# Score products of two heads in alternation between the halves of the array, and a decode result turned by 128-column transposes

## The chip, the cores and the metric

The kernel runs on one core of a Trainium2 chip. The metric is the device time of one execution in microseconds (us). Before the change it is 2710.97 us, the median of three runs (2708.78 to 2711.12). One further execution was profiled; every row of the trace is from that one. In the rows, PE is the matrix engine (TensorE), PEld its weight loads, DVE the vector engine, ACT the scalar engine, POOL GpSimd, and SP the engine that issues DMAs. L139 is line 139 of the kernel.

## The reference, cut to what matters

One layer of an encoder on 512 prompt frames and on eight decode streams of 16 frames, with float32 values throughout:

```
qa, ka, va, qb, kb, vb = split(rmsnorm(x) @ w_in)      # 16 heads A; 16 query, 2 key/value heads B; head size 64
A: softmax(qa ka^T / 8 + bias[distance]) va            # own chunk of 64 frames and the eight before
B: softmax(rope(qb) rope(kb)^T / 8, with a sink) vb    # own chunk and the two before
x = x + [rms(A) | rms(B)] @ w_out
y = rmsnorm(x + (silu(h @ w_gate) * (h @ w_up)) @ w_down),  h = rmsnorm(x)
```

The decode frames do the same against cached keys and values. The keys and values of the frames are outputs too.

## The kernel before

**Products.** A float32 operand is split into a high and a low part (`split`, L137: ACT makes the high part at L138, DVE the rest at L139), and one product is three matmuls, high by high, high by low and low by high (`mm3`, L145, lines 147, 148 and 149), or two where one operand is exact enough (`mm2`, L151, lines 154 and 155). Wherever such a helper records an operation, its line stands for all callers.

**Stages.** First the joint projection: 26 blocks of 128 columns, each through `dense` (L165), which goes over 16 blocks `k` of the contraction and issues six matmuls of 320 columns for each. Blocks 24 and 25 (keys and values of B) come first; then, for p from 0 to 7, `project_b(2p)` and `project_b(2p+1)` while p is below 4, and `project_a(p)` with three blocks. Then w_out (lines 714 and 772), and the feed-forward part, by far the longest.

**Attention inside the projections.** `dense` calls `pump` after each `k`, so once in six matmuls. `pump` (L72) takes the next of its streams and runs the generator that is active there up to its next `yield`. Up to p = 4 there are two streams, "heads 0" and "heads 1", which draw from one queue; from p = 4 on one stream takes heads and the other decode work. `heads_of` (L429) queues one generator per head, `prompt_a` (L361) or `prompt_b` (L397); `rr` is the parity of the head: an even head's 64 rows of q and k lie on partitions 0 to 63, an odd one's on 64 to 127.

A generator of A takes eleven turns: fetch the bias; scores of the query blocks 0 and 3; of 1 and 2; softmax; three empty turns; transposes of weights (`flip`, L348) in two turns; the rest of them and the first product with v; the other products. One of B takes ten. Scores (`scores`, L325) of block i are one `mm3` into one PSUM bank, 128(i+1) columns wide for A and at most 256 for B, and a DVE operation (L330) that adds the bias and takes the maximum. PSUM buffers for all this come from a pool of four banks (`bank`, L131); `dense` has its own.

`n.get` and `n.put` hand out named SBUF slots. List S has 62; 7 serve as constants, 3 for projection results, 32 hold the normalised input until the projections end, and 4 go to the queries of B, so 16 are left for heads and decode work. When a list is empty, `get` calls `pump` until another generator gives a slot back.

**Decode.** `decode_b` and `decode_a(0)` are added at p = 4, `decode_a(1)` before w_out. Ahead of w_out stands `n.drain_queue("decode")` (L708), which pumps without a projection beside it until the first two are done. `decode_a` makes for each of eight streams a block `od` with eight heads beside each other and needs, of column group t, 32 columns turned: four matmuls against a slice of the identity (L615) give 32 columns each in one bank, and two DVE copies (L620) pick 16 of each.

The order of the instructions on each engine isn't that of the source: it is chosen when the program is built, among the instructions that count as ready by then, with the source's order as priority. The first fence of the prediction that shows `x2` is an instance.

Of the kernel before, what the change touches and what calls it, by code (L numbers as in the profile page):

```python
# [8 lines left out]
ALU = mybir.AluOpType  # L9
# [4 lines left out]
P = 128  # L14
# [4 lines left out]
SP = 512  # L19
# [3 lines left out]
DS = 16  # L23
# [26 lines left out]
class Net:  # L50


    def __init__(self, nc, tc, io, pools):
        self.nc, self.tc, self.io, self.pools = nc, tc, io, pools
        self.uid = 0
        self.lists = {"S": [f"S{i}" for i in range(N_S)], "W": [f"W{i}" for i in range(N_W)]}
        self.owner, self.turns = {}, {}
        self.queues, self.active, self.turn = {}, {}, 0
        self.streams = (("heads 0", "heads"), ("heads 1", "heads"))

    def nm(self, s):
        self.uid += 1
# [159 lines left out]
def sh(t, *shape):  # L222
    v = t[:, :int(np.prod(shape))]
    if len(shape) == 2:
        v = v.rearrange("p (a b) -> p a b", a=shape[0])
    elif len(shape) == 3:
        v = v.rearrange("p (a b c) -> p a b c", a=shape[0], b=shape[1])
    return v


def r(ap):
    return ap.bitcast(F32R)


def build(nc, tc, io, pools):
    n = Net(nc, tc, io, pools)
    dma = nc.sync.dma_start
# [4 lines left out]
    def col(k):  # L242
        c0[0] += k
        return cst[:, c0[0] - k:c0[0]]
# [3 lines left out]
    sinks, sink_d = col(16), col(2)  # L248
# [4 lines left out]
    def tr(out, src):  # L253
        nc.tensor.transpose(out, src, n.ident)  # L254
# [21 lines left out]
    kb = (r(kb0), r(kb1))  # L276
# [6 lines left out]
    first = []  # L283
    for kt in range(KT):
        if kt in START_CHUNKS:
            idx, k0, k1, lst = START_CHUNKS[kt]
# [3 lines left out]
        own, hl = pair("S")  # L290
# [31 lines left out]
        return out  # L322


    def scores(q, k, rr, i, k0, k1, bias, s, mx):  # L325
        ps = n.bank()[:, :k1 - k0]
        rows = slice(64 * rr, 64 * rr + 64)
        qs, ks = slice(128 * i, 128 * i + 128), slice(k0, k1)
        n.mm3(ps, (q[0][rows, qs], q[1][rows, qs]), (k[0][rows, ks], k[1][rows, ks]), True, True)
        nc.vector.tensor_tensor_reduce(s, ps, bias, 1.0, -3e38, ALU.add, ALU.max, mx)  # L330

    def softmax(ss, mx, sink):
        nm, den = n.small(4), n.small(4)
        if sink is None:
            nc.vector.tensor_scalar(nm, mx, -1.0, None, ALU.mult)
        else:
            nc.vector.tensor_scalar(nm, mx, sink, -1.0, ALU.max, ALU.mult)
        for i, s in enumerate(ss):
            nc.scalar.activation(s, s, AF.Exp, bias=nm[:, i:i + 1], accum_out=den[:, i:i + 1])
        if sink is not None:  # L340
            se = n.small(4)
            nc.scalar.activation(se, nm, AF.Exp, bias=sink)
            nc.vector.tensor_tensor(den, den, se, ALU.add)
        nc.vector.reciprocal(den, den)
        for i, s in enumerate(ss):
            nc.vector.tensor_scalar(s, s, den[:, i:i + 1], None, ALU.mult)
# [11 lines left out]
        n.split(ps, *hl)  # L358
        return own, hl

    def prompt_a(h, q, k, v, ot, done):  # L361
        rr = h % 2
        bias, t0, t1 = n.get("S"), n.get("S"), n.get("S")
        dma(out=bias[:, :SP], in_=io["bias_a"][h])
        yield
        es = [t0[:, 512:640], t1[:, :256], t1[:, 256:640], t0[:, :512]]
        mx = n.small(4)
        for pick in ((0, 3), (1, 2)):
            for i in pick:
                scores(q, k, rr, i, 0, P * (i + 1), bias[:, SP - P * (i + 1):SP], es[i], mx[:, i:i + 1])  # L370
            yield
        softmax(es, mx, None)
        n.put("S", bias)
        yield
        yield
        yield
        yield
        blk = lambda i, j: es[i][:, P * j:P * j + P]
        o0, p0 = flip([blk(i, 0) for i in range(4)], "S")
        yield  # L380
        o1, p13 = flip([blk(i, 1) for i in range(1, 4)] + [blk(3, 3)], "S")
        yield
        ps = n.bank()
        vr = v[rr]
        n.mm2(ps, vr[:, 0:128], p0, True, False)
        n.put("S", *o0)
        o2, p2 = flip([blk(i, 2) for i in range(2, 4)], "S")
        n.put("S", t0, t1)
        yield
        n.mm2(ps[:, 128:], vr[:, 128:256], cut(p13, 0, 384), False, False)  # L390
        n.mm2(ps[:, 384:], vr[:, 384:512], cut(p13, 384, 512), False, False)
        n.mm2(ps[:, 256:], vr[:, 256:384], p2, False, True)
        n.put("S", *o1, *o2)
        both(ot, rr, ps)
        done()

    def prompt_b(t, rr, q, ot, done):  # L397
        sink = sinks[:, 8 * rr + t:8 * rr + t + 1]
        t0, t1 = n.get("S"), n.get("S")
        es = [t0[:, 512:640], t0[:, :256], t0[:, 256:512], t1[:, :256]]  # L400
        mx = n.small(4)
        for pick in ((0, 1), (2, 3)):
            for i in pick:
                k0 = max(0, i - 1) * P
                w = (i + 1) * P - k0
                scores(q, kb, rr, i, k0, k0 + w, mask_b[:, 256 - w:], es[i], mx[:, i:i + 1])
            yield
        softmax(es, mx, sink)
        yield
        yield  # L410
        yield
        yield
        oa, pa = flip([es[0], es[1][:, :P], es[2][:, P:], es[3][:, :P]], "S")
        yield
        ob, pb = flip([es[1][:, P:], es[2][:, :P], es[3][:, P:]], "S")
        n.put("S", t0, t1)
        yield
        ps = n.bank()
        vr = r((vb0, vb1)[rr])
        n.mm2(ps[:, 0:256], vr[:, 0:128], cut(pa, 0, 256), True, False)  # L420
        n.mm2(ps[:, 256:512], vr[:, 256:384], cut(pa, 256, 512), False, False)
        yield
        n.mm2(ps[:, 128:384], vr[:, 128:256], cut(pb, 0, 256), False, False)
        n.mm2(ps[:, 384:512], vr[:, 384:512], cut(pb, 256, 384), False, True)
        n.put("S", *oa, *ob)
        both(ot, rr, ps)
        done()

    def heads_of(kind, p, held, *args):  # L429
        ot = n.get("S")  # L430
        left = [2]

        def done():
            left[0] -= 1
            if not left[0]:
                dma(out=(oa_d if kind is prompt_a else ob_d)[p, :, :SP], in_=ot[:, :SP])
                n.put("S", ot)
                for lst, t in held:
                    n.put(lst, t)

        for rr in range(2):
            n.add("heads", kind(*((2 * p + rr,) if kind is prompt_a else (p, rr)), *args, ot, done))

    def rope(x):
        rot = n.get("S")
# [88 lines left out]
    def decode_a(g):  # L534
        o_s, bias, z = n.get("D"), n.get("D"), (n.get("D"), n.get("D"))
# [4 lines left out]
        for i in range(3):  # L540
            s, two = n.get("S"), (n.get("D"), n.get("D"))
# [5 lines left out]
            else:  # L547
                ps = n.bank().rearrange("p (a b) -> p a b", a=4)
# [7 lines left out]
        for b in range(NB):  # L556
            own = slice(DS * b, DS * b + DS)
            for e in range(2):
                zv = r(sh(z[e], 4, 160))
                for rr in range(2):  # L560
                    rows = slice(64 * rr, 64 * rr + 64)
# [5 lines left out]
            ps = n.bank()[:, :CA + DS]  # L567
            for hf in range(2):
# [7 lines left out]
                for j in range(2):  # L576
                    t = 2 * hf + j
# [3 lines left out]
            mx, den, d2 = n.small(1), n.small(1), n.small(1)  # L581
            s, pt = n.get("S"), n.get("S")
# [27 lines left out]
            od = n.get("S")  # L610
            nc.vector.tensor_scalar(od[:, :512], po, den, None, ALU.mult)
            yield
            pf = n.bank()[:, :P].rearrange("p (t c) -> p t c", t=4)
            for t in range(4):
                nc.tensor.matmul(pf[:, t], od[:, P * t:P * t + P], n.ident[:, 32 * t:32 * t + 32],  # L615
                                 start=True, stop=True)
            n.put("S", od)
            for rr in range(2):
                rows = slice(64 * rr, 64 * rr + 64)
                nc.vector.tensor_copy(sh(o_s, 4, P)[rows, :, own], pf[rows, :, DS * rr:DS * rr + DS])  # L620
        dma(out=oa_d[4 * g:4 * g + 4, :, SP:].rearrange("t p c -> p t c"), in_=sh(o_s, 4, P))
        n.put("D", o_s, bias, *z, *held)

# [12 lines left out]
    ps = n.bank()[:, :P]  # L636
# [38 lines left out]
    for p in range(8):  # L675
        if p < 4:
            project_b(2 * p)
            project_b(2 * p + 1)
        if p == 4:
            while len(n.lists["Q"]) < 4:  # L680
                n.pump()
            n.move("Q", "D", 4)
            n.put("D", cos, sin)
            while n.active.get("heads 1"):
                n.pump()
            n.streams = (("heads 0", "heads"), ("decode", "decode"))
            n.add("decode", decode_b())
            n.add("decode", decode_a(0))
        project_a(p)
# [24 lines left out]
    for m in range(KT):  # L714
        ps = n.dense([(io["w_out_b"][m], 8)], acts_b)
        if m == 0:
            n.rstd(ssq, 1024, r_b)
        xr, x = n.get("S"), n.get("S")
# [53 lines left out]
    for i, m in enumerate(m for kt in range(8) for m in (kt, kt + 8)):  # L772
        ps = n.dense([(io["w_out_a"][m], 8)], acts_a)
# [103 lines left out]
    for i in range(NPAIR):  # L877
        for src in ("w_gate", "w_up"):
# [4 lines left out]
            start, end = i == 0 and src == "w_gate", i == NPAIR - 1 and src == "w_up"  # L883
# [29 lines left out]
            else:  # L913
                for x, g in zip(y, gate):
                    nc.vector.tensor_tensor(x, x, g, ALU.mult)
                u, w = gate
# [211 lines left out]
```

## Time and profile before

| what | value |
|---|---|
| median of the runs | 2710.97 us |
| the profiled execution's own time | 2706.72 us |
| its span, first to last instruction | 2705.0 us |
| PE busy, DVE busy, ACT busy | 97%, 71%, 40% of the span |
| mean granted clock of PE | 0.986 |
| score products (64 rows, L147 to L149, w/o decode) | first at 81.2 us, last at 735 us |
| L615, the turning of the decode result | 128 instructions, 558.1 to 846.2 us |

A row of the timeline has the start in us, the duration in us, the engine, the line, the operation, output and inputs, the part of the array as rows x columns, the size of the moving operand, and a count of merged instructions. A duration of a matmul contains its filling and draining, so matmuls overlap; what one costs is the distance from its start to the next start.

### The profile page before, as it was taken

Reading aid. Unit: us, or ns where it says so; the run is one execution under the profiler, and the core shown is the slowest. Engines: PE = TensorE matmul, PEld = TensorE weight load, DVE = VectorE, ACT = ScalarE, POOL = GpSimd, SP = SyncE. Lnnn points to the kernel's source line nnn. Section 1 sums busy time; section 2 is a strip of 40 time slices with the busy share of each in tenths; the row PEclk is TensorE's granted clock in tenths of the full one; section 3 lists DMA queues with packets and bytes.
Section 4 is the critical chain, followed back from the end, with each engine's and each line's share of the span. In section 5 each row is a group of like instructions: output and inputs, shape, how many; then the busy total and the mean of one; then the engine's idle time right before and its main releaser. Section 6 shows DMA issues by size and latency. Waiting matters only on the chain.

```text
span 2705.0 us, 44972 instructions
## 1 busy us (share of the span) xinstructions
PE 2629.3 (97%) x17629; PEld 2568.5 (95%) x17629; DVE 1928.6 (71%) x2956; ACT 1084.0 (40%) x1759; POOL 786.9 (29%) x564
## 2 busy tenths in 40 slices
PE   7999999999999999999999999999999999999986
PEld 7999999999899999999999999999999899999986
DVE  7565565665766777667767666676668888888897
ACT  4333343444633553333333333333334444444443
POOL 3000000000211123343333333433334534444453
PEclk9999999999999999999999999999999899999997
DMA  5222223333556443333333333333335644444344
GB/s 166 85 73 82 89 68 108 109 119 114 183 187 217 147 134 104 104 119 103 105 115 108 108 121 100 119 102 109 113 106 173 214 130 127 132 133 130 107 116 135
DMA packets 154147, 332.23 MB, mean 123 GB/s; under 512 B 18064, under 2 KB 69264, under 8 KB 153936
## 3 DMA queue, kind: packets, MB, share of 16 engines
q1 hardware_dynamic: 153936, 329.38, 38.8%
q8 instruction: 138, 2.26, 0.4%
q14 instruction: 73, 0.60, 0.1%
HBM read 274.38 MB, written 54.20 MB: 121 GB/s over the span
## 4 chain that ended last, share of the span: by engine, by line
PE 84%; DVE 8%; DMA 4%; issue 3%; ACT 2%; SPq 0%; DVEq 0%; POOL 0%; ACTq 0%
PE dn L147 18%; PE dn L149 17%; PE dn L148 17%; PE at L147 9%; PE at L149 9%; PE at L148 9%; DVE W L139 2%; PE at L254 1%; DVE S L847 1%; DMA S<-act_d 1%; DMA W<-w_down 1%; DVE S L139 1%; PE at L155 1%; PE at L154 1%; DVE S L1018 0%
## 5 line engine op out<-in xcount | busy, mean ns | idle before, releaser
L147 PE MATMUL dn<-S,W 128*128 128x320 f32 x3694 | 1165.9, 316 | 15.4 <-DVE S L847 9.6
L149 PE MATMUL dn<-S,W 128*128 128x320 f32 x3694 | 1152.1, 312 | 14.0 <-DVE W L139 13.8
L148 PE MATMUL dn<-S,W 128*128 128x320 f32 x3694 | 1150.3, 311 | 1.1 <-DVE S L139 1.1
L138 ACT ACTIVATE W<-W 128x1024 fp32r<-128x1024 f32 (+2 forms) x632 | 609.3, 965 | 1045.1 <-PE dn L148 518.0
L139 DVE TENSOR_TENSOR W<-W,W 128x1024 fp32r<-128x1024 f32 (+2 forms) x632 | 768.3, 1216 | 126.6 <-ACT W L138 122.3
L147 PEld LDWEIGHTS dn<-S,W 128*128 128x128 f32 x3694 | 700.6, 190 | 33.2 <-issue 16.9
L149 PEld LDWEIGHTS dn<-S,W 128*128 128x128 f32 x3694 | 700.3, 190 | 19.4 <-DVE W L139 18.9
L148 PEld LDWEIGHTS dn<-S,W 128*128 128x128 f32 x3694 | 701.1, 190 | 3.0 <-DVE S L139 1.3
L149 PE MATMUL at<-S,W 128*128 128x320 f32 x1594 | 494.4, 310 | 7.0 <-DVE W L139 6.6
L147 PE MATMUL at<-S,W 128*128 128x320 f32 x1594 | 493.5, 310 | 1.5 <-ACT W L138 1.5
L148 PE MATMUL at<-S,W 128*128 128x320 f32 x1594 | 493.0, 309 | 0.0
L830 POOL TENSOR_TENSOR W<-W,W 128x1024 f32<-128x1024 f32 (+2 forms) x76 | 162.5, 2138 | 588.0 <-DVE W L139 519.0
L149 PEld LDWEIGHTS at<-S,W 128*128 128x128 f32 x1594 | 299.5, 188 | 10.2 <-DVE W L139 10.2
L147 PEld LDWEIGHTS at<-S,W 128*128 128x128 f32 x1594 | 299.9, 188 | 1.7 <-ACT W L138 1.7
L148 PEld LDWEIGHTS at<-S,W 128*128 128x128 f32 x1594 | 299.6, 188 | 0.0
L847 DVE TENSOR_TENSOR S<-S,dn 128x320 f32<-128x320 f32 x358 | 164.2, 482 | 97.6 <-PE dn L149 97.6
L826 DVE TENSOR_TENSOR W<-W,W 128x1024 f32<-128x1024 f32 (+2 forms) x76 | 134.5, 1770 | 103.9 <-DMA W<-w_up 52.4
L837 POOL TENSOR_TENSOR W<-W,W 128x1024 f32<-128x1024 f32 (+2 forms) x76 | 165.5, 2178 | 111.9 <-DVE W L139 106.5
L847 DVE TENSOR_TENSOR S<-S,at 128x320 f32<-128x320 f32 x262 | 123.5, 481 | 70.1 <-PE at L149 70.0
L218 POOL TENSOR_TENSOR S<-S,S 128x640 f32<-128x640 f32 x40 | 75.7, 1893 | 155.5 <-ACT S L217 155.1
L828 DVE TENSOR_TENSOR W<-W,W 128x1024 f32<-128x1024 f32 (+2 forms) x76 | 82.9, 1091 | 30.7 <-DMA W<-w_gate 24.1
L139 DVE TENSOR_TENSOR S<-at,S 128x512 fp32r<-128x512 f32 (+2 forms) x109 | 64.1, 600 | 50.3 <-ACT S L138 49.9
(149 smaller groups left out, 2351.0 us busy)
## 6 DMA issues: line engine op xcount, KB each, us to landing
W<-w_gate SPq DMA_DIRECT2D x88, 512.0 KB
W<-w_up SPq DMA_DIRECT2D x88, 512.0 KB
W<-w_in SPq DMA_DIRECT2D x66, 512.0 KB
W<-w_down SPq DMA_DIRECT2D x64, 384.0 KB
W<-w_down SPq DMA_DIRECT2D x68, 320.0 KB
act_d<-S SPq DMA_DIRECT2D x66, 320.0 KB
half<-act_d SPq DMA_DIRECT2D x81, 160.0 KB
S<-act_d SPq DMA_DIRECT2D x80, 160.0 KB
```

Of the source, the lines that this page charges most:

```text
L138: self.nc.scalar.activation(hi, src, AF.Identity)
L139: self.nc.vector.tensor_tensor(lo, src, f(hi), ALU.subtract)
L147: mm(out, a[0], b[0], start=first, stop=False)
L148: mm(out, a[0], b[1], start=False, stop=False)
L149: mm(out, a[1], b[0], start=False, stop=last)
L154: mm(out, a, b[0], start=first, stop=False)
L218: (eng or nc.gpsimd).tensor_tensor(ssq, ssq, sq, ALU.add)
L826: nc.vector.tensor_tensor(b12[:, w], b12[:, w], b22[:, w], sub)
L828: nc.vector.tensor_tensor(s6[:, w], b11[:, w], b12[:, w], sub)
L830: nc.gpsimd.tensor_tensor(b11[:, w], b22[:, w], s6[:, w], sub)
L837: nc.gpsimd.tensor_tensor(b21[:, w], b21[:, w], s6[:, w], sub)
L847: add = lambda o, a, b: nc.vector.tensor_tensor(o, a, b, ALU.add)
```

## The change

A generator now serves two heads, an even and an odd one. `scores` takes both, gets two banks, and issues the six matmuls in alternation, so that neighbours in the order use different halves of the array's rows. Blocks of A go from the widest to the narrowest, one block of both heads per turn. The softmax of the two heads takes two turns; two empty turns follow (there were three); the tails of the two heads take turns (`in_turn`). There is one stream of heads up to p = 4, where there were two, and the wait for "heads 1" at p = 4 goes.

The decode result is turned by four plain 128-column transposes into a whole bank, and the two copies read the wanted 16 columns of each group through a view with a step of 160 columns (`diagonal`).

```
-        self.streams = (("heads 0", "heads"), ("heads 1", "heads"))
+        self.streams = (("heads 0", "heads"),)
...
+def diagonal(ap, first):
+
+    return bass.AP(tensor=ap.tensor, offset=ap.offset + first, ap=[list(ap.ap[0]), [160, 4], [1, DS]])
...
-    def scores(q, k, rr, i, k0, k1, bias, s, mx):
-        ps = n.bank()[:, :k1 - k0]
-        rows = slice(64 * rr, 64 * rr + 64)
+    def scores(q, k, i, k0, k1, biases, ss, mxs):
+
+        pss = [n.bank()[:, :k1 - k0] for _ in range(2)]
         qs, ks = slice(128 * i, 128 * i + 128), slice(k0, k1)
-        n.mm3(ps, (q[0][rows, qs], q[1][rows, qs]), (k[0][rows, ks], k[1][rows, ks]), True, True)
-        nc.vector.tensor_tensor_reduce(s, ps, bias, 1.0, -3e38, ALU.add, ALU.max, mx)
+        for x, (a, b) in enumerate(((0, 0), (0, 1), (1, 0))):
+            for rr, ps in enumerate(pss):
+                rows = slice(64 * rr, 64 * rr + 64)
+                nc.tensor.matmul(ps, q[a][rows, qs], k[b][rows, ks], start=x == 0, stop=x == 2)
+        for ps, bias, s, mx in zip(pss, biases, ss, mxs):
+            nc.vector.tensor_tensor_reduce(s, ps, bias, 1.0, -3e38, ALU.add, ALU.max, mx[:, i:i + 1])
+
+    def in_turn(works):
+
+        while works:
+            for w in list(works):
+                try:
+                    next(w)
+                    yield
+                except StopIteration:
+                    works.remove(w)
...
+        for i in (3, 2, 1, 0):
+            w = P * (i + 1)
+            scores(q, k, i, 0, w, [x[:, SP - w:SP] for x in biases], [h[1][i] for h in heads], [h[2] for h in heads])
+            yield
+        n.put("S", *biases)
+        for _, es, mx in heads:
+            softmax(es, mx, None)
+            yield
         yield
         yield
-        yield
-        yield
+        yield from in_turn([tail_a(rr, own, es, v, ot, done) for rr, (own, es, _) in enumerate(heads)])
...
-            pf = n.bank()[:, :P].rearrange("p (t c) -> p t c", t=4)
+            pf = n.bank()
             for t in range(4):
-                nc.tensor.matmul(pf[:, t], od[:, P * t:P * t + P], n.ident[:, 32 * t:32 * t + 32],
-                                 start=True, stop=True)
+                tr(pf[:, P * t:P * t + P], od[:, P * t:P * t + P])
...
-                nc.vector.tensor_copy(sh(o_s, 4, P)[rows, :, own], pf[rows, :, DS * rr:DS * rr + DS])
+                nc.vector.tensor_copy(sh(o_s, 4, P)[rows, :, own], diagonal(pf[rows], DS * rr))
...
-            while n.active.get("heads 1"):
-                n.pump()
```

`prompt_b` is changed in the same way as `prompt_a`, with blocks 0 to 3 in this order. Turns per pair of heads: 16 for A (two generators of eleven before) and 15 for B (two of ten).

More of the change, by code (lines that the diff above doesn't have):

```diff
@@ L359, in flip, with prompt_a, tail_a @@
         return own, hl
[L361 to L364, printed above, removed]
+    def prompt_a(p, q, k, v, ot, done):
+        biases = n.get("S"), n.get("S")
+        for rr, bias in enumerate(biases):
+            dma(out=bias[:, :SP], in_=io["bias_a"][2 * p + rr])
         yield
[L366 to L370, printed above, removed]
+        heads = []
+        for rr in range(2):
+            t0, t1 = n.get("S"), n.get("S")
+            heads.append(((t0, t1), [t0[:, 512:640], t1[:, :256], t1[:, 256:640], t0[:, :512]], n.small(4)))
+        for i in (3, 2, 1, 0):
+            w = P * (i + 1)
+            scores(q, k, i, 0, w, [x[:, SP - w:SP] for x in biases], [h[1][i] for h in heads], [h[2] for h in heads])
             yield
-        softmax(es, mx, None)
-        n.put("S", bias)
+        n.put("S", *biases)
+        for _, es, mx in heads:
+            softmax(es, mx, None)
+            yield
         yield
         yield
-        yield
-        yield
+        yield from in_turn([tail_a(rr, own, es, v, ot, done) for rr, (own, es, _) in enumerate(heads)])
+    def tail_a(rr, own, es, v, ot, done):
         blk = lambda i, j: es[i][:, P * j:P * j + P]
@@ L387, in prompt_a @@
         o2, p2 = flip([blk(i, 2) for i in range(2, 4)], "S")
-        n.put("S", t0, t1)
+        n.put("S", *own)
         yield
@@ L395, in prompt_a, with prompt_b, tail_b @@
         done()
[L397 to L406, printed above, removed]
+    def prompt_b(t, q, ot, done):
+        heads = []
+        for rr in range(2):
+            t0, t1 = n.get("S"), n.get("S")
+            heads.append(((t0, t1), [t0[:, 512:640], t0[:, :256], t0[:, 256:512], t1[:, :256]], n.small(4)))
+        for i in range(4):
+            k0 = max(0, i - 1) * P
+            w = (i + 1) * P - k0
+            scores(q, kb, i, k0, k0 + w, [mask_b[:, 256 - w:]] * 2, [h[1][i] for h in heads], [h[2] for h in heads])
             yield
-        softmax(es, mx, sink)
+        for rr, (_, es, mx) in enumerate(heads):
+            softmax(es, mx, sinks[:, 8 * rr + t:8 * rr + t + 1])
+            yield
         yield
         yield
-        yield
-        yield
+        yield from in_turn([tail_b(rr, own, es, ot, done) for rr, (own, es, _) in enumerate(heads)])
+    def tail_b(rr, own, es, ot, done):
         oa, pa = flip([es[0], es[1][:, :P], es[2][:, P:], es[3][:, :P]], "S")
@@ L415, in prompt_b @@
         ob, pb = flip([es[1][:, P:], es[2][:, :P], es[3][:, P:]], "S")
-        n.put("S", t0, t1)
+        n.put("S", *own)
         yield
@@ L439, in done @@
                     n.put(lst, t)
-        for rr in range(2):
-            n.add("heads", kind(*((2 * p + rr,) if kind is prompt_a else (p, rr)), *args, ot, done))
+        n.add("heads", kind(p, *args, ot, done))
     def rope(x):
```

## The prediction, made before the changed kernel was run

> **What bounds the kernel now.** I read the page first, then PE's busy time by stage, then PE's order of time inside the attention stages.
>
> ```profile
> span 2705.0 us, 44972 instructions
> PE 2629.3 (97%) x17629; PEld 2568.5 (95%) x17629; DVE 1928.6 (71%) x2956; ACT 1084.0 (40%) x1759; POOL 786.9 (29%) x564
> PE 84%; DVE 8%; DMA 4%; issue 3%; ACT 2%; SPq 0%; DVEq 0%; POOL 0%; ACTq 0%
> ```
>
> ```profile
> 80.00:430.00 350.00, 349.12 (x2368) 331.34 (x2368) 206.29 (x508) 138.38 (x326) 4.96 (x12) 1.00 0.26 84
> 430.00:690.00 260.00, 258.20 (x1737) 240.62 (x1735) 162.39 (x446) 112.55 (x264) 14.61 (x53) 1.00 0.37 115
> 690.00:700.00 10.00, 8.63 (x54) 7.54 (x53) 7.31 (x12) 6.92 (x12) 6.32 (x7) 1.00 0.82 279
> 700.00:712.00 12.00, 11.22 (x52) 9.58 (x51) 10.03 (x20) 7.85 (x15) 8.13 (x7) 0.72 0.67 198
> 1200.00:1300.00 100.00, 100.00 (x684) 100.00 (x683) 68.03 (x73) 34.02 (x36) 37.66 (x21) 1.00 0.34 111
> ```
>
> PE holds 84% of the chain that ended last, and it is busy for 349.12 of 350 us and 258.20 of 260 us in the two stretches of attention beside projections. DVE has a share of 59% and 62% there. So what PE is spared there comes off the end, and waiting elsewhere costs nothing until it reaches PE. The last row is dense work alone: 100/684 = 0.146 us from one 320-column matmul to the next, and 0.88 us for the six between two pumps. Only 690 to 712 us is worse: little is at hand between the last projection and w_out, and the clock granted in 700 to 712 is 0.72.
>
> **What a score turn costs.** Turns are single blocks inside dense work. Cost: from the last dense start before it to the second after it, less two periods (0.29 us).
>
> ```profile
> 144.89 0.31 PE L149 MATMUL dn<-S,W 128*128 128x320 f32 x1
> ...
> 145.80 0.39 PE L148 MATMUL at<-W,W 64*128 64x512 f32 x1
> 146.04 0.39 PE L149 MATMUL at<-W,W 64*128 64x512 f32 x1
> ...
> 146.61 0.31 PE L148 MATMUL dn<-S,W 128*128 128x320 f32 x1
> ...
> 149.49 0.31 PE L149 MATMUL dn<-S,W 128*128 128x320 f32 x1
> ...
> 150.37 0.33 PE L148 MATMUL at<-W,W 64*128 64x384 f32 x1
> 150.55 0.33 PE L149 MATMUL at<-W,W 64*128 64x384 f32 x1
> ...
> 151.06 0.31 PE L148 MATMUL dn<-S,W 128*128 128x320 f32 x1
> ...
> 199.96 0.31 PE L149 MATMUL dn<-S,W 128*128 128x320 f32 x1
> ...
> 201.33 0.31 PE L148 MATMUL dn<-S,W 128*128 128x320 f32 x1
> ...
> 201.91 0.31 PE L149 MATMUL dn<-S,W 128*128 128x320 f32 x1
> ...
> 203.31 0.31 PE L148 MATMUL dn<-S,W 128*128 128x320 f32 x1
> ```
>
> A's first turn (128 and 512 columns) costs 1.72 - 0.29 = 1.43 us, its second (256 and 384) 1.57 - 0.29 = 1.28; B's cost 1.37 - 0.29 = 1.08 and 1.40 - 0.29 = 1.11. With 16 heads each: A 16 x 2.71 = 43.4, B 16 x 2.19 = 35.0, together 78.4 us on the path. A 512-column matmul starts 0.24 us after the one before, a 384-column one 0.18.
>
> Do two halves of the array run beside each other? The trace of before already has places where an even and an odd head stand next to each other:
>
> ```profile
> 437.87 0.31 PE L149 MATMUL dn<-S,W 128*128 128x320 f32 x1
> 438.11 0.19 PEld L147 LDWEIGHTS at<-S,S 64*128 64x128 f32 x2 [0.19 <-issue]
> 438.11 0.34 PE L147 MATMUL at<-S,S 64*128 64x144 f32 x2
> ...
> 438.28 0.28 PE L148 MATMUL at<-S,S 64*128 64x144 f32 x2
> ...
> 438.39 0.28 PE L149 MATMUL at<-S,S 64*128 64x144 f32 x2
> ...
> 438.85 0.31 PE L148 MATMUL dn<-S,W 128*128 128x320 f32 x1
> ...
> 103.13 0.29 PE L148 MATMUL at<-S,S 64*128 64x256 f32 x2
> 103.25 0.29 PE L149 MATMUL at<-S,S 64*128 64x256 f32 x2
> ```
>
> The first is decode_b's two halves: "x2" in 0.28 us, where one alone takes as long, and the two weight loads lie in one 0.19 us as well. Six matmuls cost 0.98 - 0.29 = 0.69 us: three steps of 0.11, and 0.36 that is left for entering and leaving the 64-row form. The last two rows are heads of B, 256 columns wide, stepping by 0.12 in pairs. (Decode_b's source issues one half's three and then the other's: the built order mixes them, so alternation survives the ordering.)
>
> **The change, part by part.** *Scores.* 64 turns stay 64 turns (four for each of 16 pairs), so 0.36 stays; the six matmuls take three steps. A's turns: 0.36 + 3 x 0.24 = 1.08, + 3 x 0.18 = 0.90, + 3 x 0.12 = 0.72, + 3 x 0.11 = 0.69, sum 3.39 against 5.42 for two heads. B's: 0.69 + 3 x 0.72 = 2.85 against 4.38. Saved 8 x 2.03 + 8 x 1.53 = 28.5 us; the first two pairs of B overlap partly already (103.13 is one), for which I take off 1.5: **-27.0 us**. Pairs of 384 and 512 columns aren't in the trace: at best they step like single ones (taken, as 256 does), at worst one after the other, and then A saves only 6 us and the sum is -17.
>
> *Decode result.* Sixteen times, beside dense work in both stages:
>
> ```profile
> 650.40 0.31 PE L149 MATMUL dn<-S,W 128*128 128x320 f32 x1
> 650.55 0.97 PE L615 MATMUL at<-cst,S 128*128 128x32 f32 x8
> ...
> 651.59 0.30 PE L148 MATMUL dn<-S,W 128*128 128x320 f32 x1
> ...
> 212.91 0.31 PE L149 MATMUL dn<-S,W 128*128 128x320 f32 x1
> 213.06 0.60 PE L254 MATMUL at<-cst,S 128*128 128x128 f32 x4
> ...
> 213.64 0.30 PE L148 MATMUL dn<-S,W 128*128 128x320 f32 x1
> ```
>
> Four matmuls appear as eight and cost 1.19 - 0.29 = 0.90 us; four transposes cost 0.73 - 0.29 = 0.44. Saved 16 x 0.46 = **-7.4 us**. The two copies keep their 64x64 elements:
>
> ```profile
> L620 DVE COPY S<-at 64x64 f32<-64x64 f32 x32 | 7.1, 222 | 12.1 <-PE at L615 11.8
> ```
>
> Should the longer step cost them half as much again, that is 3.6 us on DVE, hidden by its 38% of idle time; exposed, it would only delay the write to `oa_d`.
>
> The Trainium skill, "TensorE: Matmul & The Clock Gate", Part 4, states about 275 ns for a 128x128 transpose within a kernel. Taken as a price each, four would cost 1.10 us and this part would add 3.2 us. The trace has four in 0.60 us, a new one each 0.11 us, so it doesn't bear the rule out as a price; it is a rival below.
>
> *Lead of the softmax.* A wait that grows. From the last score turn to the first transpose a head had five of its own turns, hence ten of `dense` with two streams; now it is five of `dense` up to p = 4.
>
> ```profile
> 153.66 0.17 DVE L335 TENSOR_SCALAR sm<-sm 128x4 f32<-128x4 f32 x1
> ...
> 154.26 1.28 DVE L346 TENSOR_SCALAR S<-S,sm 128x128 f32<-128x128 f32 x4
> ...
> 156.45 1.27 DVE L346 TENSOR_SCALAR S<-S,sm 128x128 f32<-128x128 f32 x4
> 157.64 1.22 DVE L139 TENSOR_TENSOR W<-W,W 128x1024 fp32r<-128x1024 f32 x1
> ```
>
> The first head's last score matmul is the 150.55 one above; its weights are scaled at 154.26 + 1.28 = 155.5, 5.0 us later, the second head's 2.2 us after that. Lead after the change: 0.36 (150.55 to 151.06, less one period) + 5 x 0.88 = 4.8 us for the first, and one turn with four transposes more, 0.88 + 0.44, for the second: 6.1. So they are 0.2 and 1.1 us late by this count. Queued on PE behind a late transpose are the dense matmuls, and behind them all. If PE stood still, 11 pairs (eight of B, three of A before p = 4) would lose 12 us, and with a weight split (the 1.22 us of L139) ahead on DVE 26 us. If dense work is ordered ahead, nothing. I take **+2.5**, near that end, because the built order follows readiness. From p = 4 on heads alternate with decode work, the lead is 9 us, and it suffices.
>
> *Fewer turns.* Decode_b and decode_a(0) need 113 turns. Four rounds of 48 pumps leave them 4 x (48 - 22) = 104 now, and nine are pumped bare at L708 in the poor stretch 690 to 712. With 16 turns on heads, taken alternately, they get 4 x (48 - 16) = 128: the bare pumping goes. What is late next are the operands of w_out, split by ACT and DVE as the input's slots come free. Bounds: all of the idle time and of the low clock of that stretch, -6 us (1.37 + 0.78 + 0.28 x 12 = 5.5), and +8, eight operands by 1 us of DVE with nothing on PE. I take **-2**.
>
> *Slots.* From p = 4 on 16 slots of S serve both streams. One head held seven at most (two, four for two pairs of halves, one output), decode work six. A pair holds 13, so `get` will pump out of turn. Each of four or five pairs may lose one or two turns' order, 0 to 8 us; **+2**, as dense work lies beside it. DMA issues are the same in number; on SP two bias loads of a pair stand together, a turn and more ahead of use.
>
> Sum: -27.0 - 7.4 + 2.5 - 2 + 2 = **-31.9 us**. The profiled execution took 2706.72 us, so 2674.8; it lies 4.25 below the median, and on the median's scale the forecast is 2710.97 - 31.9 = **2679.1 us**.
>
> **Rivals.** *Only part of the overlap.* If weight loads come one at a time (0.11 each), six cost 0.66: turns of 1.02, and 1.08 at 512; A saves 1.28 and B 0.30 a pair, 12.6 in all, giving 2693. If the wide ones don't overlap, 2689. Against both: pairs of loads within one 0.19 us, and 256 columns in pairs.
>
> *The halves don't alternate* (no bank for the second head at that time, so dense work comes between): only decode's 7.4 less 2.5 stays, 2706. Against it: four banks as now, and two per turn as now.
>
> *Transposes at full price:* 2679.1 + 7.4 + 3.2 = 2690.
>
> *Slower: the softmax chain kept in source order.* If DVE runs the second head's maximum behind the first one's scaling, that head starts its 0.17, its exponentials (2.2, the distance of the two scalings) and its 1.27 only at 5.0 us, is ready at 8.6, 2.5 late, and 3.7 with a weight split ahead: 11 x 3.7 = 41 us on PE, 2679.1 - 2.5 + 41 = 2718. It decides against the change from 34.4 / 11 = 3.1 us a pair. Against it: the quoted L335 is the second head's, and it runs before the first head's scaling.
>
> **How the numbers follow.** Forecast 0.73 (2668 to 2692 by its bounds), partial overlap 0.11, transposes 0.03, no alternation 0.06, slower 0.07. The low end of the range is all of the gains without the costs (-27.0 - 7.4 - 6 = -40.4) and a little; the upper one takes in the partial overlaps with 6 us more of late transposes, 2699. 0.2% (5.4 us) is about what a measurement of this kernel tells from none. Faster: the first three, 0.87; same: no alternation, 0.06; slower 0.07.
>
> **What would show it.** Right: score rows "x2" everywhere, turns of 1.08, 0.90, 0.72 and 0.69 us; four transposes of 0.44 us in the place of L615; the last projection ending some 28 us earlier than now (2 x 7 + 10.7 of scores, half of decode's gain); PE at 99% up to there. Wrong: matmuls of one half only between dense ones; 512-column pairs stepping by 0.48; transposes or dense matmuls waiting for L346 or L139 for a microsecond or more in each pair; idle PE at w_out's begin beyond the 2 us it has now.

## The result, and the profile after

The changed kernel takes 2687.55 us (median of four runs, 2684.86 to 2689.5); the kernel before, beside it, 2709.88 (2706.22 to 2711.12). The ratio is 0.992, its 95% interval 0.9908 to 0.9932: faster by 22.3 us. The forecast was 31.9. The profiled execution took 2686.44 us against 2706.72, so it gained 20.3.

The page of the kernel after: span, busy time by engine, and the chain that ended last, by engine.

```profile
span 2684.7 us, 44841 instructions
PE 2602.1 (97%) x17565; PEld 2545.6 (95%) x17565; DVE 1930.3 (72%) x2956; ACT 1081.6 (40%) x1759; POOL 785.4 (29%) x564
PE 64%; DVE 5%; DMA 2%; issue 2%; ACT 1%; POOL 0%; SPq 0%; DVEq 0%; POOLq 0%; ACTq 0%
```

PE lost 64 instructions, the second half of each turning multiplication, and 27.2 us of busy time. Its share of the chain, 64% instead of 84%, doesn't say that PE bounds the kernel less: the shares add up to 74%, because the chain could be followed back only to 693.53 us, where it begins with an operand split on DVE. What changed is read from the stretches. Columns as before: window, length, busy time of PE, PEld, DVE, ACT and POOL, granted clock, DMA share, GB/s.

```profile
80.00:428.00 348.00, 343.04 (x2387) 327.17 (x2387) 204.14 (x510) 136.26 (x326) 5.63 (x13) 0.99 0.27 85
428.00:690.00 262.00, 258.58 (x1762) 238.98 (x1761) 177.60 (x468) 124.74 (x286) 24.13 (x63) 1.00 0.39 125
680.00:690.00 10.00, 10.00 (x70) 10.00 (x70) 10.00 (x8) 8.62 (x14) 7.54 (x5) 1.00 0.86 297
690.00:700.00 10.00, 4.10 (x22) 3.58 (x21) 9.91 (x11) 3.63 (x7) 6.76 (x4) 0.76 0.58 211
700.00:712.00 12.00, 12.00 (x80) 10.56 (x80) 7.79 (x21) 4.63 (x7) 1.17 (x5) 0.91 0.58 194
```

Two things are new. While heads share the projections (up to 428 us) PE is idle for 4.96 us; before, it was 0.88. And between 690 and 700 us PE works for 4.1 us of ten, where it had 8.63, while DVE is busy for 9.91.

The halves do run side by side. PE's order of time in a pair of A:

```profile
143.92 0.31 PE L149 MATMUL dn<-S,W 128*128 128x320 f32 x1
144.16 0.97 PE L337 MATMUL at<-W,W 64*128 64x512 f32 x6
...
145.31 0.31 PE L148 MATMUL dn<-S,W 128*128 128x320 f32 x1
...
145.90 0.31 PE L149 MATMUL dn<-S,W 128*128 128x320 f32 x1
146.13 0.79 PE L337 MATMUL at<-W,W 64*128 64x384 f32 x6
...
147.11 0.30 PE L148 MATMUL dn<-S,W 128*128 128x320 f32 x1
...
193.10 0.31 PE L149 MATMUL dn<-S,W 128*128 128x320 f32 x1
193.44 0.44 PE L337 MATMUL at<-S,S 64*128 64x128 f32 x4
194.16 0.73 PE L337 MATMUL at<-S,S 64*128 64x128 f32 x8 [0.29 <-DVE S L139]
194.82 0.42 PE L147 MATMUL dn<-S,W 128*128 128x320 f32 x1
195.08 0.30 PE L148 MATMUL dn<-S,W 128*128 128x320 f32 x1
195.85 1.79 PE L337 MATMUL at<-S,S 64*128 64x256 f32 x12 [0.47 <-DVE sm L339]
...
198.00 0.47 PE L147 MATMUL dn<-S,W 128*128 128x320 f32 x1
198.27 0.47 PE L148 MATMUL dn<-S,W 128*128 128x320 f32 x1
```

Six matmuls of 512 columns cost 145.31 - 143.92 - 0.29 = 1.10 us, six of 384 columns 0.92; the two narrower turns of A cost 0.74 and 0.68. That is 3.44 a pair, where 3.39 was forecast. In the starts of the single matmuls the overlap shows directly: of A's 192 score matmuls none starts within 0.025 us of another one before, and all 192 do after.

A pair of B looks otherwise. The one shown is the worse kind, three of the eight: its four turns come in two blocks of twelve matmuls with two dense ones between, and twice PE stands still, once for the split of a query (L139) and once for a maximum that frees a bank (L339). The other five come as one block of 24 matmuls. In such piles the halves partly fall out of step: 146 of B's 192 matmuls start together with another one, 46 alone. After the second block dense matmuls start 0.27 us apart instead of 0.146, and the clock granted up to 428 us is 0.99.

Here is what every kind of work on PE cost, as the sum of the distances from each start to the next, from the first instruction to the last result of w_out's group b (880.5 us before, 863.5 after). It is worked out from the starts in the two traces; a wait counts with the work before it.

```
us                            before    after
score products                  65.3     45.6   -19.7
turning (transposes, L615)      49.5     42.7    -6.8
dense work                     645.0    654.5    +9.5
weights by v (two products)     36.0     37.3    +1.3
decode products                 71.2     69.2    -2.0
norms and the rest               5.8      6.5    +0.7
sum                            872.8    855.8   -17.0
```

The last result of group b thus comes 17.0 us earlier. Of the rise in dense work 6.2 us are one step, from 692.18 to 698.34 us, the idle stretch before w_out. The other 3.3 us of the span's 20.3 lie behind group b, in the feed-forward part, which the change doesn't touch. Single executions differ by as much: in a second profiled execution of the kernel after, with nothing changed, group b's last result comes at 861.3 us, and what follows it is 2.1 us longer than in the first.

### The profile page after: what moved, and what is told of

Same layout as the page of the kernel before. It is cut to its first block, busy times and chain, and to the rows that moved or that the text cites. A ratio compares the mean times of both kernels' runs of the same rounds, so it can differ in the third digit from the quotient of the medians.

```text
span 2684.7 us, 44841 instructions
## 1 busy us (share of the span) xinstructions
PE 2602.1 (97%) x17565; PEld 2545.6 (95%) x17565; DVE 1930.3 (72%) x2956; ACT 1081.6 (40%) x1759; POOL 785.4 (29%) x564
## 4 chain that ended last, share of the span: by engine, by line
PE 64%; DVE 5%; DMA 2%; issue 2%; ACT 1%; POOL 0%; SPq 0%; DVEq 0%; POOLq 0%; ACTq 0%
PE dn L149 13%; PE dn L147 13%; PE dn L148 13%; PE at L149 8%; PE at L148 8%; PE at L147 8%; DVE W L139 2%; DVE S L869 1%; DMA S<-act_d 1%; DMA W<-w_down 1%; DVE S L1040 1%; PE at L259 0%; DVE S L882 0%; DVE W L850 0%; ACT W L138 0%
## 5 line engine op out<-in xcount | busy, mean ns | idle before, releaser
L147 PE MATMUL dn<-S,W 128*128 128x320 f32 x3694 | 1163.5, 315 | 14.6 <-DVE S L869 5.6
L139 DVE TENSOR_TENSOR W<-W,W 128x1024 fp32r<-128x1024 f32 (+2 forms) x632 | 770.3, 1219 | 142.3 <-ACT W L138 137.5
L218 POOL TENSOR_TENSOR S<-S,S 128x640 f32<-128x640 f32 x40 | 77.9, 1947 | 163.7 <-ACT S L217 162.9
L471 POOL MEMSET S<- 80x640 f32 x9 | 5.7, 630 | 318.9 <-PE at L155 167.1
```

The source lines that it names most:

```text
L139: self.nc.vector.tensor_tensor(lo, src, f(hi), ALU.subtract)
L147: mm(out, a[0], b[0], start=first, stop=False)
L218: (eng or nc.gpsimd).tensor_tensor(ssq, ssq, sq, ALU.add)
```

## The experiments

Each ratio is to the kernel before, run on the same chip. The kernel after was run once more, on the same chip as the order within a turn, the squares on DVE and both repairs together: 2684.78 us, ratio 0.9908 (0.9893 to 0.9923).

**The decode result alone.** The kernel before with the transposes for the decode result, and its scores as they were:

```
-                nc.tensor.matmul(pf[:, t], od[:, P * t:P * t + P], n.ident[:, 32 * t:32 * t + 32],
-                                 start=True, stop=True)
+                tr(pf[:, P * t:P * t + P], od[:, P * t:P * t + P])
```

> The kernel before with the decode result's turning alone changed. Theory (transposes step by 0.11 us, four in place of eight matmuls): 16 x 0.42 to 0.46 = 7 us less than before, about 2703 us, ratio 0.9975, and the stretch of four transposes costs 0.44 us of PE. Rival (each transpose has its full 0.27 us as a price): 3 us more than before, ratio 1.001. Rival (other work hides either form): ratio 1.000.

Measured: 2700.01 us, ratio 0.9963 (0.9949 to 0.9977), some 10 us less, with 6 to 14 by the interval, so the 7 that were forecast lie in it. By PE's starts, counted as above, turning fell from 49.5 to 42.1 us. So the price of 0.44 us for four holds, and the rival at the full price, which would have made this kernel slower, falls. In this run's one trace, though, dense work takes 3.9 us more, and group b's last result comes only 2.2 us earlier. How this fits with the 6 to 14 us of the medians stays open.

**One half a turn.** The kernel after, but a turn issues two blocks of one head, as before, and the next turn those of the other:

```
-        for i in (3, 2, 1, 0):
-            w = P * (i + 1)
-            scores(q, k, i, 0, w, [x[:, SP - w:SP] for x in biases], [h[1][i] for h in heads], [h[2] for h in heads])
-            yield
+        for pick in ((0, 3), (1, 2)):
+            for rr, (_, es, mx) in enumerate(heads):
+                for i in pick:
+                    w = P * (i + 1)
+                    scores(q, k, rr, i, 0, w, biases[rr][:, SP - w:SP], es[i], mx[:, i:i + 1])
+                yield
```

> The changed kernel with pairs, turns and streams as they are, but each turn of scores does two blocks of one head, as before the change, so that neighbours use the same half of the array. Theory (what is gained comes from two halves running beside each other): the 20 us that PE's score matmuls lost between the two traces come back, about 2707 us, ratio 0.999, with score turns of 1.08 to 1.43 us. Rival (the gain comes from fewer turns and one stream, not from the overlap): stays near 2688 us, ratio 0.992.

Measured: 2699.5 us, ratio 0.9963 (0.9951 to 0.9976), the same as the transposes alone: on balance all that the pairing of heads gives goes with this edit. Against the kernel after it is 0.0043 x 2710 = 12 us slower, where the theory had 20 and the rival none; both forecasts lie outside the interval. In the starts the scores rise from 45.6 to 63.3, by 17.7; some 6 of these come back in other work, so that 11.4 are left at group b's last result.

The run takes the overlap from A alone. None of A's 192 score matmuls starts together with another one any more, and A's turns, entry and exit included, cost 43.4 us again instead of 27.5. B's still pile up, 82 of 192 start together in the pile, and they cost 28.9 us against 29.8. Its first turn of A is this:

```profile
143.79 0.31 PE L149 MATMUL dn<-S,W 128*128 128x320 f32 x1
144.03 0.33 PE L147 MATMUL at<-W,W 64*128 64x128 f32 x1
144.19 0.27 PE L148 MATMUL at<-W,W 64*128 64x128 f32 x1
144.30 0.28 PE L149 MATMUL at<-W,W 64*128 64x128 f32 x1
144.42 0.44 PE L147 MATMUL at<-W,W 64*128 64x512 f32 x1
144.70 0.39 PE L148 MATMUL at<-W,W 64*128 64x512 f32 x1
144.93 0.39 PE L149 MATMUL at<-W,W 64*128 64x512 f32 x1
145.26 0.41 PE L147 MATMUL dn<-S,W 128*128 128x320 f32 x1
145.51 0.31 PE L148 MATMUL dn<-S,W 128*128 128x320 f32 x1
```

Each matmul stands alone ("x1"), and the turn costs 145.51 - 143.79 - 0.29 = 1.43 us, as in the kernel before.

**The order within a turn.** The kernel after with the three matmuls of one head ahead of the three of the other in the source:

```
-        for x, (a, b) in enumerate(((0, 0), (0, 1), (1, 0))):
-            for rr, ps in enumerate(pss):
+        for rr, ps in enumerate(pss):
+            for x, (a, b) in enumerate(((0, 0), (0, 1), (1, 0))):
```

> The changed kernel with the six matmuls of a turn issued in the source as three of one head and then three of the other. Theory (the order built from the source mixes two groups that use different halves, as it did with decode_b's halves): the halves still run in pairs for most turns, score turns stay within 0.2 us of the changed kernel's, and the time is within 3 us of it: ratio 0.992 to 0.993. Rival (the source's order decides): turns of 1.1 to 1.7 us as with one half a turn, about 2700 us, ratio 0.9965.

Measured: 2689.84 us, ratio 0.9928 (0.9915 to 0.994), 2 us above the first measurement of the kernel after and 5 above the second, on the same chip; the intervals overlap, so a difference isn't shown. Its turns of A cost 1.10, 0.92, 0.76 and 0.68 us, and all 192 matmuls start together with another one: the order that is built mixes the halves by itself, as it did with decode_b before. What counts is that both heads' products are at hand in one turn, and not the alternation that the source writes out.

**B ten turns later.** In the kernel after the sixteen turns of a pair of A, or the fifteen of a pair of B, fill the sixteen pumps of one `project_b`, so the next pair of B begins its scores in the first turns of the block behind it. Its query isn't there yet. DVE's order of time, the multiplication of the projected block (L326), the three rotations (L475 to L477) and the split:

```profile
182.77 0.82 DVE L326 TENSOR_TENSOR S<-dn,S 128x640 f32<-128x640 f32 x1 [0.38 <-PE dn L149]
...
188.96 0.81 DVE L475 TENSOR_TENSOR S<-S,S 80x640 f32<-80x640 f32 x1
...
190.51 0.82 DVE L476 TENSOR_TENSOR S<-S,S 80x640 f32<-80x640 f32 x1
191.37 0.82 DVE L477 TENSOR_TENSOR S<-S,S 80x640 f32<-80x640 f32 x1
...
193.42 0.69 DVE L139 TENSOR_TENSOR S<-S,S 128x512 fp32r<-128x512 f32 x1 [0.70 <-ACT S L138]
```

The split ends 11.3 us after the multiplication began. The four turns of scores, due from the block's first pump on, have all come up by then, and they go off at once. With 22 turns of A ahead, as before, B's scores came at least six turns later. This kernel puts ten empty turns ahead of them:

```
     def prompt_b(t, q, ot, done):
+        for _ in range(10):
+            yield
         heads = []
```

> The changed kernel with ten empty turns at the head of each pair of B. Theory (B's score turns come due before their rotated queries exist, so they pile up into blocks of 12 and 24 matmuls without dense work between, and wait for PSUM banks): with the turns later, each is a single block of 0.69 to 0.75 us, a pair costs 2.9 us where the changed kernel's trace has 3.2 to 4.3, and 5 to 7 us go: about 2681 us, ratio 0.9895. Rival (a pile costs nothing on balance, since it enters and leaves the 64-row form once, not four times): 2686 to 2689 us, ratio 0.992.

Measured: 2678.54 us, ratio 0.9885 (0.9871 to 0.9898), 9.5 us less than the kernel after by the ratios (6.2 by its second measurement); in the traces group b's last result comes 9.9 us earlier (7.7 against the second trace). B's turns now stand singly in dense work, all but the first three, and 190 of 192 matmuls start together with another one:

```profile
264.33 0.31 PE L149 MATMUL dn<-S,W 128*128 128x320 f32 x1
264.57 0.63 PE L337 MATMUL at<-S,S 64*128 64x128 f32 x6
...
265.37 0.31 PE L148 MATMUL dn<-S,W 128*128 128x320 f32 x1
...
265.95 0.31 PE L149 MATMUL dn<-S,W 128*128 128x320 f32 x1
266.19 0.62 PE L337 MATMUL at<-S,S 64*128 64x256 f32 x6
...
267.00 0.31 PE L148 MATMUL dn<-S,W 128*128 128x320 f32 x1
```

The two cost 265.37 - 264.33 - 0.29 = 0.75 and 0.76 us, four of them 2.9 a pair where 2.85 was forecast. In the kernel after a pair costs between 3.25 and 4.32, 29.8 for all eight pairs; here all eight cost 23.8. In the attention stage up to p = 4 the scores fall from 32.4 to 25.8 us and the products of weights by v from 24.5 to 22.5; PE's idle time there is 0.24 of 337 us.

```profile
80.00:417.00 337.00, 336.76 (x2377) 316.45 (x2376) 202.31 (x508) 136.33 (x326) 4.96 (x12) 1.00 0.27 88
```

**Where the idle stretch before w_out comes from.** PE's order of time in the kernel after, the only long wait in the attention stages:

```profile
692.18 0.31 PE L147 MATMUL dn<-S,W 128*128 128x320 f32 x1
698.34 1.11 PE L259 MATMUL at<-cst,S 128*128 128x128 f32 x4 [5.85 <-DVE S L326]
```

The last of the projection's blocks (34 with B's queries, not 26) starts its last matmul on PE at 690.84 us; the dense ones behind it, up to the 692.18 above, are w_out's first. The block's multiplication on DVE (L326) begins only at 697.47, because w_out's operands are ahead of it on that engine. DVE, and POOL beside it:

```profile
683.81 5.11 DVE L143 SCALAR_TENSOR_TENSOR S<-S,cst,S 128x640 fp32r<-128x640 f32 x3
688.85 2.59 DVE L139 TENSOR_TENSOR W<-W,W 128x1024 fp32r<-128x1024 f32 x1
691.36 4.24 DVE L143 SCALAR_TENSOR_TENSOR S<-S,cst,S 128x640 fp32r<-128x640 f32 x2
695.62 1.93 DVE L139 TENSOR_TENSOR S<-S,S 128x512 fp32r<-128x512 f32 x1
697.47 0.81 DVE L326 TENSOR_TENSOR S<-dn,S 128x640 f32<-128x640 f32 x1
```

```profile
683.86 13.14 POOL L218 TENSOR_TENSOR S<-S,S 128x640 f32<-128x640 f32 x6 [0.95 <-ACT S L217]
```

While POOL adds six squares of the operands (L218), the last two splits with gain on DVE (L143) take 4.24 / 2 = 2.1 us each. I had two ways of meeting this.

*More turns.* The kernel after with six more empty turns in each pair of A from p = 3 on, so that the pairs pump as often as two heads did and decode work is left over for the stretch:

```
-        yield
-        yield
+        for _ in range(2+(6 if p >= 3 else 0)):
+            yield
```

> The changed kernel with six more empty turns in each pair of A that runs beside decode work, so that a pair takes 22 turns as two heads did before, decode work is later again, and nine of its turns are pumped bare ahead of w_out. Theory (the 5.9 us in which PE waits at 692 us for the last projection's multiplication, which stands behind operand splits on DVE, is exposed because no decode work is left to fill it): the hole shrinks to under 2 us, but the bare turns' own waits come back, so 2 to 5 us less than the changed kernel: 2683 to 2686 us, ratio 0.991. Rival (filler doesn't matter, the multiplication is as late with it): 2687 us or more, the hole stays.

Measured: 2684.64 us, ratio 0.9911 (0.9897 to 0.9924), not to be told from the kernel after. The wait for L326 shrinks to 0.5 us, but a wait of 2.1 us for ACT (L611) comes some 45 us later, and the decode work that was held back costs the w_out stage what the hole did: the first result of w_out comes 1.5 us earlier, but group b's last at 863.4 us instead of 863.5. Filling the hole with deferred work moves it.

*Squares on DVE.* The kernel after with the squares of w_out's operands added by DVE:

```
-            n.add_square(ssq, o, t == 0, "S")
+            n.add_square(ssq, o, t == 0, "S", nc.vector)
```

> The changed kernel, with the sums of squares over w_out's operands added on DVE instead of POOL. Theory (the last projection's multiplication is 5 us late because the operand splits ahead of it on DVE take 2.1 us each beside POOL's adds, and 0.88 without): splits of 0.9 us, the wait of 5.8 us on PE at the end of the projections falls to 3 us or less, in spite of up to seven adds of 0.8 us more on DVE: 2 to 4 us less than the changed kernel. Rival (the splits are as slow without POOL, or the adds take the place of what they save): the wait stays at 5 to 7 us, same time.

Measured: 2677.96 us, ratio 0.9883 (0.987 to 0.9897), 6.8 us less than the kernel after on the same chip, more than I expected although DVE has more to do. The eight splits of the operands, from the view of one line (durations in ns, least, median and most; first and last start), first in the kernel after and then in this one:

```profile
L143 DVE SCALAR_TENSOR_TENSOR S<-S,cst,S x8: 872/1512/2201, 676.4 to 693.5; 128x640 fp32r<-128x640 f32 x8
```

```profile
L143 DVE SCALAR_TENSOR_TENSOR S<-S,cst,S x8: 876/884/887, 675.8 to 689.7; 128x640 fp32r<-128x640 f32 x8
```

PE's wait for L326 (us in total, times, longest) and the stretch from 690 us, both of this kernel:

```profile
PE at L259 <- DVE S L326: 1.4, 1, 1.4
```

```profile
690.00:700.00 10.00, 8.64 (x55) 6.84 (x54) 9.25 (x19) 5.04 (x9) 1.11 (x4) 1.00 0.89 295
```

The splits take 0.88 us each; in the kernel after four of the eight took 2.1 to 2.2. PE's wait falls from 5.8 to 1.4 us, by 4.4 of the 6.8 us, and the granted clock from 690 to 700 us rises from 0.76 to 1.00. Group b's last result comes at 856.8 us, 6.8 earlier than in the first trace of the kernel after and 4.6 earlier than in the second, which has the same wait of 5.8 us. So the wait is the main part; what the rest is, these traces don't settle.

*Both.* Ten empty turns ahead of B and the squares on DVE.

> Ten empty turns ahead of B's scores and the sums of squares on DVE together. Theory (two separate places): the gains add, 9 us and 2 to 4 us, 2675 to 2677 us, ratio 0.987 to 0.988. Rival (the second gain isn't there): 2678.5 us as with the empty turns alone, ratio 0.9885.

Measured: 2670.17 us (2669.24 to 2671.82), ratio 0.9856 (0.9843 to 0.987): 38.5 us less than the kernel before, the best of all, and 5 us below the forecast, which had the squares at 2 to 4 us. On one chip it is 14.6 us less than the kernel after, and the two gains were 6.2 to 9.5 and 6.8: they add up, so neither repair hides the other.

## Why the prediction was right, and where it was not

The direction was right, the time lies in the range, and two thirds of the size came. That the range held is partly luck: it reached so far up for halves that overlap only in part and for late transposes, and neither came, while the pile-up of B that took most of the missing gain wasn't in it. Of the signs of being wrong one came, more idle PE at w_out's begin. The steps one by one:

**The overlap of the halves: right.** Where turns stand singly, they cost what was forecast, at 384 and 512 columns as well, which the trace of before didn't show. A saves 8 x (5.42 - 3.44) = 15.8 us; 16.2 were forecast. Both partial rivals (loads one at a time, wide matmuls one after the other) and "the halves don't alternate" fall.

**B's scores: the step that failed.** "Turns are single blocks inside dense work" was read off the kernel before and carried over, and B's term of 8 x 1.53, less 1.5, rested on it. With entry and exit included, B's scores cost about 33.9 us before and 29.8 after, so they saved some 4 instead of 10.7. The same text counted that pairs of heads take fewer turns, and priced only what this does to decode work. That it also brings B's scores forward, to a time when their query is still being rotated, was not in the sum. B ten turns later shows both the cause and the size: single turns again, 6.0 us off the cost of B's scores, and 6.2 to 9.5 off the time.

**The decode result: right.** -7.4 forecast, -6.8 in PE's starts (-7.3 with this part alone), and the copies are as fast as before:

```profile
L644 DVE COPY S<-at 64x64 f32<-64x64 f32 x32 | 7.1, 221 | 6.0 <-PE at L259 5.7
```

The Trainium skill, "TensorE: Matmul & The Clock Gate", Part 4, gives about 275 ns for a 128x128 transpose in one kernel; transposes here last 280 ns on average, so the trace agrees with it as a duration. As a price each it doesn't hold: four cost 0.44 us here.

**Lead of the softmax, +2.5: didn't come.** In the waits of PE there is none for the scaling of weights (L365). That the built order puts dense work ahead of a transpose that isn't ready fits this, but no run took it apart. The slower rival, the chain in source order, falls.

**Fewer turns, -2 with -6 and +8 as bounds: right in kind, wrong in sign.** The bare pumping went, and nine more turns of decode work are done before the last projection ends. What was late next were the operands of w_out, as the upper bound said, "eight operands by 1 us of DVE with nothing on PE". By the prediction's own working the stretch from 690 to 712 us lost 5.5 us before; now it loses 5.90 of idle time, and 0.24 x 4.1 and 0.09 x 12 of clock, 8.0 in all. So -2 became +2.5. The bound had the right queue, but not what made it long: POOL's adds, beside which the splits take up to 2.2 us.

**Slots, +2:** not separable. Waits of a few tenths of a microsecond beside decode work are there; no experiment took them apart.

**The last projection's end, 28 us earlier:** wrong. The block's last matmul on PE starts 6.6 us earlier than before (690.8 against 697.4) and its multiplication, L326, 1.8 (697.5 against 699.3). B's pile-up and the decode work moved ahead of this point stand before both, and the slow splits before L326; how much each takes wasn't measured. The first result of w_out is 18.3 us earlier. The mark was badly chosen, since the forecast itself moved decode work across it.

Added up as measured, A (-15.8), B (-4), the decode result (-7) and the queue (+2.5) give -24, where the medians have 22.3, and group b's last result 17.0 in the first trace and 19.2 in the second.

Not settled: why the profiled executions after are 1 to 5 us shorter behind group b than the one before, of which 2.1 is what two executions of one kernel differ by, and how the gain of the transposes alone divides.

## What to carry to other kernels

Pair work that uses different halves of the array's rows so that both are at hand at one time; the written alternation isn't needed where the build chooses the order. When work takes fewer turns, ask of everything queued behind it whether its operands are there that much earlier, and put empty turns back just where they aren't. A hole at the seam of two stages is closed on the engine whose queue delays the first operand, and not by saving filler for it.

## What the runs showed of the hardware

DVE and POOL held each other up. A split with two inputs in SBUF that takes 0.88 us without them took up to 2.2 beside POOL's adds, one of 1024 columns 2.59 instead of 1.22, one of 512 columns 1.93 instead of 0.69: at worst 1.2 to 1.4 us more, whatever its length, while the six adds took 13.14 / 6 = 2.19 us each, where the fastest in this kernel takes 1.56. With the adds on DVE the splits were back at 0.88. The Trainium skill, "SBUF — State Buffer", section "Who interferes with whom", says that a VectorE instruction with two inputs in SBUF and a GpSimd instruction that reads SBUF exclude each other, the later one waiting for the earlier to end. The constant addition fits that, though it is somewhat less than a whole add.

A short stall can cost more than its length, and need not. After the 0.47 us wait in the pair of B above, dense matmuls start 0.27 us apart, with a granted clock of 0.50 from 198 to 200 us, and so they do after the wait of 5.85 us, with 0.50 from 698 to 702. But in the second profiled execution of the same kernel the same wait stands in the same pair of B, and the clock granted behind it stays at 1.00:

```profile
197.15 1.51 PE L337 MATMUL at<-S,S 64*128 64x256 f32 x12 [0.47 <-DVE sm L339]
...
198.85 0.31 PE L147 MATMUL dn<-S,W 128*128 128x320 f32 x1
199.00 0.31 PE L148 MATMUL dn<-S,W 128*128 128x320 f32 x1
```

So part of what the pile-up costs changes from one execution to the next, and with it part of the 9.9 us in the traces of B ten turns later.
